# The projections of a two-layer mixer and expert block: three float32r products a step, or one float32 product

## The chip, the cores and the metric

The kernel runs on one core of a Trainium2 chip. The metric is the device time of one execution in microseconds (us), the median of several runs. The engines are named as the profile names them: PE (TensorE, the matrix products, with its weight loads as PEld), DVE (VectorE), ACT (ScalarE), POOL (GpSimd) and SP (SyncE, which here only issues DMA loads).

## The reference, cut to what matters

The input is 256 tokens of 1024 channels in float32. Two layers follow one another, and each has two halves:

```python
h = modulate(rms_norm(x, g_mix[l]), sh1, sc1)
x = x + g1 * token_mixers(h, pos, w_in[l], ..., w_o[l])
h = modulate(rms_norm(x, g_ffn[l]), sh2, sc2)
x = x + g2 * grouped_moe(h, w_router, b_router, w_gate[l], w_up[l], w_down[l])

def token_mixers(h, pos, w_in, w_dw, b_dw, ln_g, ln_b, w_o):
    proj = h @ w_in                                   # 256 x 1024 by 1024 x 2340
    cu, cg, dq, dk, dv, iq, ik, iw, mq, mk, mv = jnp.split(proj, offs, axis=-1)
    y_conv = conformer_conv(cu, cg, w_dw, b_dw, ln_g, ln_b)   # 31 taps, 256 channels
    ...                                               # rope on dq, dk, iq, ik, mq, mk
    y_dsa = dsa_attention(dq, dk, dv, iq, ik, iw)     # 6 heads; each query keeps its top 64 keys
    y_moba = moba_attention(mq, mk, mv)               # 6 heads; one block here, so causal
    return jnp.concatenate([y_conv, y_dsa, y_moba], axis=-1) @ w_o    # 1024 x 1024
```

The vectors `sh1`, `sc1`, `g1` and their like come from a product of `silu(c)` with `w_ada`. `grouped_moe` runs 16 experts with gate, up and down matrices; a router gives each token two of them. The two products of `token_mixers`, with `w_in` and with `w_o`, are what the change touches.

## The kernel before

Time goes through these stages: the product with `w_ada`, the mixers of layer 0 (about 35 to 169 us in the profile), the experts of layer 0, the mixers of layer 1 (about 324 to 459 us), the experts of layer 1, and the last norm.

**Weights.** All of them (181 MB, float32) pass through one ring of 14 slots of SBUF. The list `loads` fixes their order. `pump()` lets SP issue the next load (L77) as long as a slot is free, and `done(key)` gives a slot back once all that read it have read it, and pumps again. A mixer stage takes from the ring two slots of `ix`, eight slots of 256 columns of `w_in` (`cu`, `cg`, `d0`, `d1`, `q0`, `q1`, `m0`, `m1`) and four slots of `w_o`; an expert pair takes four slots of gate and up and two of `w_down`. The loads of the experts come right behind those of the mixers.

**Split products.** The mixers' products are in the type float32r. An operand is split in a high part, its cast to float32r, and a low part, what the cast leaves of it, and three products stand for one: high by high, high by low, low by high. For weights `split()` does it: ACT casts a piece of the ring slot to `WH` (L404), POOL subtracts that from the slot and leaves `WL` (L405). Each has four buffers.

```python
S.copy(WH, w)
G.tensor_tensor(WL, w, WH.bitcast(F32), OP.subtract)
```

The activations are split where they are made: `hH` on ACT (L416), `hL` on DVE (L417). The mixers' results go the same way into `yH` and `yL`, in `Pair.value` (L567, L568) and behind the convolution (L729, L730).

**Products of the mixers.** `proj` makes tokens by columns, `proj_T` (for `cu` and `cg`) columns by tokens. Each goes over eight rows of 128 (`k`) and two blocks of the result, which are 16 steps of three products each (L442 to L444, L459 to L461). A product has 256 columns, in `ix` 292. `out_part(k)` adds the part of `w_o` that belongs to row block `k` of the result `y` to eight accumulators: eight steps of three products (L664 to L666), and eight parts in a layer, so 64 steps.

**Attention.** Results of a projection are copied from PSUM by ACT, turned by the rope on DVE (`rope_in_place`, L474 to L477, two blocks of tokens with four operations each), transposed on PE (`transposes`, L483) and copied into the buffer `QK` by DVE (L484). A `Pair` is two heads: `score` (the products in `score_mm`, L493 and L495, and the softmax, whose row minima are DVE's at L533, exponentials ACT's at L536, reciprocal DVE's at L539, scaling DVE's at L543), `flip` (transposes of the probabilities on PE, L551) and `value`. For the dsa heads `select_keys` first finds the top 64 scores of each query in eight rounds on DVE. `score_mm` has the index products as well.

**Convolution.** Its 31 taps are DVE operations over 256 columns, for two blocks of channels (the first tap of a block at L692, the others at L694, together 56 in a layer). The last six taps of the second block are POOL's: one product (L681), then five sums (L685) of terms that ACT makes (L684); they are called `rest` and are added at L700. A mean over channels (L706, L718) is a float32 product on PE.

**What sets the order.** In `mixers` the order on PE is that of the code, by hand: `ix`, `cu`, transposes of the index heads, `cg`, the index scores, then `d0`, `d1`, `q0`, first flip, `q1`, second flip, `early.take` (products with `w_ada` for a later stage), third flip, `dsa[0].score`, `m0`, and so on, at the end the parts of the output projection with flips and scores of the moba heads between them. The order on DVE, ACT and POOL is set by a scheduler when the program is built, by its own costs; the taps have no place of their own and fill in where it thinks that DVE has nothing else. In the expert stage the orders of PE and of DVE are both by hand.

Of the kernel before, what the change touches and what calls it, by code (L numbers as in the profile page):

```python
# [52 lines left out]
def block_kernel(ctx: ExitStack, tc: tile.TileContext, x, c, w_ada, b_ada, g_mix, w_in, w_dw, b_dw, ln_conv_g,  # L53
# [346 lines left out]

    def split(wk, w, shape):
        WH = wk.tile(shape, F32R, name="WH", tag="WH", bufs=4)
        WL = wk.tile(shape, F32R, name="WL", tag="WL", bufs=4)
        S.copy(WH, w)  # L404
        G.tensor_tensor(WL, w, WH.bitcast(F32), OP.subtract)  # L405
        return WH, WL

    def mixers(big, wk, l, norm, early):
        a1, sh1 = mod["sc1", l], mod["sh1", l]
        rs = norm.rs  # L410
        hH = big.tile([P, KT, SEQ], F32R, name="hH", tag="H")
        hL = big.tile([P, KT, SEQ], F32R, name="hL", tag="L")
        for k in range(KT):
            t = wk.tile([P, SEQ], F32, name="ht", tag="ht")
            V.scalar_tensor_tensor(out=t, in0=xT[:, k, :], scalar=a1[:, k:k + 1], in1=rs, op0=OP.mult, op1=OP.mult)
            S.activation(hH[:, k, :], t, AF.Identity, bias=sh1[:, k:k + 1])  # L416
            V.scalar_tensor_tensor(out=hL[:, k, :], in0=t, scalar=sh1[:, k:k + 1], in1=hH[:, k, :].bitcast(F32),  # L417
                                   op0=OP.add, op1=OP.subtract)
        QK = big.tile([P, 10, SEQ], F32, name="QK")
# [7 lines left out]
        def proj(name, w=256):  # L427
            if w <= 256:
                pp = bank([P, NT, w])
                pts = [pp[:, t, :] for t in range(NT)]  # L430
            else:
                pts = [bank([P, w]) for _ in range(NT)]
                pp = pts
            for kh in range(4):
                WH, WL = split(wk, w_rows(name, 2 * kh), [P, 2, w])
                for kk in range(2):
                    k = 2 * kh + kk
                    for t in range(NT):
                        tt = slice(t * P, (t + 1) * P)
                        first = k == 0 and (w > 256 or t == 0)  # L440
                        last = k == KT - 1 and (w > 256 or t == NT - 1)
                        T.matmul(pts[t], hH[:, k, tt], WH[:, kk, :], start=first, stop=False)  # L442
                        T.matmul(pts[t], hH[:, k, tt], WL[:, kk, :], start=False, stop=False)  # L443
                        T.matmul(pts[t], hL[:, k, tt], WH[:, kk, :], start=False, stop=last)  # L444
                if name == "ix" and kh % 2 == 1:
                    done(("win", l, "ix", kh // 2))
            if name != "ix":
                done(("win", l, name))
            return pp

        def proj_T(name):
            pp = bank([P, 2, SEQ])
            for kh in range(4):
                WH, WL = split(wk, w_rows(name, 2 * kh), [P, 2, 256])
                for kk in range(2):
                    k = 2 * kh + kk
                    for cc in range(2):
                        cs = slice(cc * P, (cc + 1) * P)
                        T.matmul(pp[:, cc, :], WH[:, kk, cs], hH[:, k, :], start=(k == 0 and cc == 0), stop=False)  # L459
                        T.matmul(pp[:, cc, :], WH[:, kk, cs], hL[:, k, :], start=False, stop=False)  # L460
                        T.matmul(pp[:, cc, :], WL[:, kk, cs], hH[:, k, :], start=False, stop=(k == KT - 1 and cc == 1))  # L461
            done(("win", l, name))
# [55 lines left out]
        class Pair:  # L518
# [40 lines left out]
            def value(self):  # L559
# [4 lines left out]
                for i, v in enumerate((va, vb)):  # L564
                    T.matmul(po[64 * i:64 * i + 64, P:2 * P], v[1], self.pts[i][:, 2 * P:3 * P], start=False,
                             stop=True)
                S.copy(yH[:, dst, :], po)  # L567
                V.tensor_tensor(yL[:, dst, :], po, yH[:, dst, :].bitcast(F32), OP.subtract)  # L568

# [66 lines left out]
        pp = proj("m1")  # L636
        yH = big.tile([P, KT, SEQ], F32R, name="yH", tag="H")
        yL = big.tile([P, KT, SEQ], F32R, name="yL", tag="L")
        S.copy(VV[:, :, HD:HD + 256], pp)
# [17 lines left out]
        def out_part(k):  # L657
            ki = nk[0]
            for n in range(KT):
                if n % 4 == 0:  # L660
                    WH, WL = split(wk, wt["wo", l, k // 2][:, k % 2, n * P:(n + 4) * P], [P, 512])
                ns = slice((n % 4) * P, (n % 4 + 1) * P)
                po = pos[n // 2][:, n % 2, :]
                T.matmul(po, WH[:, ns], yH[:, k, :], start=(ki == 0 and n % 2 == 0), stop=False)  # L664
                T.matmul(po, WH[:, ns], yL[:, k, :], start=False, stop=False)  # L665
                T.matmul(po, WL[:, ns], yH[:, k, :], start=False, stop=(ki == KT - 1 and n % 2 == 1))  # L666
            nk[0] += 1
# [55 lines left out]
        for cc in range(2):  # L723
# [4 lines left out]
        V.scalar_tensor_tensor(out=yc, in0=th, scalar=1.0, in1=yc, op0=OP.add, op1=OP.mult)  # L728
        S.activation(yH[:, 0:2, :], yc, AF.Copy, scale=0.5)  # L729
        V.scalar_tensor_tensor(out=yL[:, 0:2, :], in0=yc, scalar=0.5, in1=yH[:, 0:2, :].bitcast(F32), op0=OP.mult,  # L730
                               op1=OP.subtract)
        out_part(4)
# [603 lines left out]
```

## Time and profile before

| | us |
|---|---|
| three runs | 607.84, 608.03, 612.25 |
| their median | 608.03 |
| the profiled execution | 609.77 |
| its span (first to last instruction) | 608.1 |
| mean granted clock of PE in it | 0.946 |
| PE busy | 535.8 |
| DVE busy | 348.2 |
| ACT busy | 215.8 |
| POOL busy | 181.1 |

The profiled execution is 1.7 us longer than its span, and 0.3% longer than the median of the runs. The costliest line on POOL is L405, the subtraction, with 138.0 us in 104 operations; on ACT it is L404, the cast, with 62.5 us. The products of L442 to L444 and L664 to L666 are float32r; those of `score_mm`, the transposes and the means are float32. A group of equal instructions that follow one another is drawn together in a timeline row, with its count (x12), and the time from the start of the first to the end of the last. A float32 product is recorded as two matmuls, so two products stand there as x4. The granted clock is a share of the full one, 2.4 GHz; the lower level is 1.2 GHz, so 0.5.

### The profile page before, as it was taken

To read this page: it belongs to the slowest core of one execution; us is meant where nothing else is said; L and a number is where in the kernel's file an instruction comes from. 1 tells how busy PE (TensorE), PEld (TensorE's weight loads), DVE (VectorE), ACT (ScalarE), POOL (GpSimd) and SP (SyncE) were. 2 spreads that over 40 slices of the span, in tenths; PEclk is the share of its full clock that TensorE was granted. 3 is DMA by queue.
4 is the path that set the end of the run, shared out by engine and by line. 5 is a ranking of instruction groups with operands and counts; after the bars stand their busy time and mean duration, and the time that the engine had idled before them with its cause. 6 is when DMAs were issued, how large, how long until landed. Compare 5 with 4: busy or idle time off the path is not lost. (4 is left out here: it accounts for less than half of the span.)

```text
span 608.1 us, 11533 instructions
## 1 busy us (share of the span) xinstructions
PE 535.8 (88%) x4297; PEld 341.3 (56%) x4297; DVE 348.2 (57%) x912; ACT 215.8 (35%) x472; POOL 181.1 (30%) x155
## 2 busy tenths in 40 slices
PE   2788979599979999999968997697998899999993
PEld 0268975468945355555436797383895444444431
DVE  1275899987575332333237689999756733333323
ACT  0353713366661212111146372244676121111114
POOL 1056738333630000000005775533362011111110
PEclk9788979699998999999978997898999899999998
DMA  8999988948289999999999998745637699999952
GB/s 319 380 304 386 393 321 314 376 137 265 87 254 365 365 359 359 357 358 362 391 362 370 386 386 325 274 141 152 213 120 215 219 349 354 363 357 356 360 202 73
DMA packets 126027, 182.85 MB, mean 301 GB/s; under 512 B 7920, under 2 KB 94216, under 8 KB 125960
## 3 DMA queue, kind: packets, MB, share of 16 engines
q1 hardware_dynamic: 125344, 180.80, 86.2%
q10 hardware_dynamic: 616, 1.19, 0.5%
q8 instruction: 38, 0.62, 0.4%
q14 instruction: 29, 0.24, 0.1%
HBM read 180.92 MB, written 1.05 MB: 299 GB/s over the span
## 5 line engine op out<-in xcount | busy, mean ns | idle before, releaser
L405 POOL TENSOR_TENSOR WL<-w,WH 128x512 fp32r<-128x512 f32 (+1 forms) x104 | 138.0, 1355 | 141.7 <-ACT WH L404 123.7
L979 PE MATMUL bank<-w,XT 128*32 128x512 f32 (+1 forms) x1024 | 112.9, 592 | 0.0
L404 ACT CAST WH<-w 128x512 fp32r<-128x512 f32 (+1 forms) x104 | 62.5, 624 | 43.5 <-PE bank L460 19.1
L979 PEld LDWEIGHTS bank<-w,XT 128*32 128x32 f32 x1024 | 33.5, 110 | 75.1 <-issue 68.4
L444 PE MATMUL bank<-WH,hL 128*128 128x256 f32 (+1 forms) x224 | 68.7, 307 | 3.0 <-DVE hL L417 2.8
L442 PE MATMUL bank<-WH,hH 128*128 128x256 f32 (+1 forms) x224 | 69.1, 308 | 1.0 <-ACT hH L416 0.9
L443 PE MATMUL bank<-WL,hH 128*128 128x256 f32 (+1 forms) x224 | 68.0, 303 | 1.2 <-POOL WL L405 1.2
L694 DVE SCALAR_TENSOR_TENSOR cvy<-cva,hw,cvy 128x256 f32<-128x256 f32 x108 | 59.3, 594 | 0.5
L1017 PE MATMUL bank<-w,eaT 128*32 128x512 f32 (+1 forms) x512 | 58.2, 595 | 0.4
L967 DVE SCALAR_TENSOR_TENSOR eac<-eth,bank 128x256 f32<-128x256 f32 x16 | 6.7, 422 | 83.4 <-ACT eth L966 83.4
L275 PE MATMUL bank<-w,cB 128*32 128x512 f32 x384 | 51.3, 652 | 3.1 <-DMA w<-in_w_ada 1.2
L444 PEld LDWEIGHTS bank<-WH,hL 128*128 128x128 f32 x224 | 46.6, 208 | 4.9 <-DVE hL L417 4.9
L442 PEld LDWEIGHTS bank<-WH,hH 128*128 128x128 f32 x224 | 47.2, 211 | 3.7 <-ACT hH L416 2.0
L443 PEld LDWEIGHTS bank<-WL,hH 128*128 128x128 f32 x224 | 46.9, 209 | 1.4 <-POOL WL L405 1.4
L1005 POOL TENSOR_TENSOR Yl<-yf,Yh 128x512 fp32r<-128x512 f32 x14 | 18.0, 1287 | 95.0 <-ACT Yh L1004 95.0
L966 ACT ACTIVATE eth<-bank 128x256 f32<-128x256 f32 x16 | 6.1, 384 | 96.2 <-PE bank L979 96.2
L1184 POOL MEMSET rc<- 128x4 f32 x2 | 0.2, 102 | 131.3 <-ACT warm L259 131.3
L664 PE MATMUL bank<-yH,WH 128*128 128x256 f32 x128 | 37.0, 289 | 0.0
L665 PE MATMUL bank<-yL,WH 128*128 128x256 f32 x128 | 35.8, 280 | 0.0
L666 PE MATMUL bank<-yH,WL 128*128 128x256 f32 x128 | 35.8, 280 | 0.0
L957 PE MATMUL bank<-D,gH 128*128 128x256 f32 x128 | 33.5, 299 | 2.4 <-DVE eac L967 2.4
L536 ACT ACTIVATE pr<-pr,nm 128x128 f32<-128x128 f32 (+1 forms) x48 | 21.3, 445 | 39.4 <-DVE nm L533 39.4
(287 smaller groups left out, 1026.4 us busy)
## 6 DMA issues: line engine op xcount, KB each, us to landing
w<-in_w_ada SPq DMA_DIRECT2D x48, 1024.0 KB, 12.0
w<-in_w_gate SPq DMA_DIRECT2D x128, 256.0 KB, 6.2
w<-in_w_up SPq DMA_DIRECT2D x128, 256.0 KB, 6.0
w<-in_w_down SPq DMA_DIRECT2D x64, 512.0 KB, 7.8
w<-in_w_in SPq DMA_DIRECT2D x16, 1024.0 KB, 13.1
w<-in_w_o SPq DMA_DIRECT2D x8, 1024.0 KB, 8.8
w<-in_w_in SPq DMA_DIRECT2D x4, 328.0 KB, 15.0
xin<-in_x ACTq DMA_DIRECT2D x1, 1024.0 KB, 9.8
```

Source lines behind the costliest of these rows:

```text
L275: T.matmul(self.pa[j:j + 32, :], cB[:, 2 * kq + kk, o:o + 32], W[:, kk, h * 512:(h + 1) * 512], start=(u == 0 and kq == 0), stop=(u + 1 == ...
L404: S.copy(WH, w)
L405: G.tensor_tensor(WL, w, WH.bitcast(F32), OP.subtract)
L442: T.matmul(pts[t], hH[:, k, tt], WH[:, kk, :], start=first, stop=False)
L443: T.matmul(pts[t], hH[:, k, tt], WL[:, kk, :], start=False, stop=False)
L444: T.matmul(pts[t], hL[:, k, tt], WH[:, kk, :], start=False, stop=last)
L664: T.matmul(po, WH[:, ns], yH[:, k, :], start=(ki == 0 and n % 2 == 0), stop=False)
L665: T.matmul(po, WH[:, ns], yL[:, k, :], start=False, stop=False)
L666: T.matmul(po, WL[:, ns], yH[:, k, :], start=False, stop=(ki == KT - 1 and n % 2 == 1))
L694: tap = V.scalar_tensor_tensor(out=cy[:, cc, :], in0=src, scalar=w, in1=cy[:, cc, :], op0=OP.mult, op1=OP.add)
L979: T.matmul(pf[b0:b0 + BLK, :], XT[:, k, o + b0:o + b0 + BLK], W[:, e, k % 2, :], start=(k == 0), stop=(k == KT - 1))
L1017: T.matmul(pd[b0:b0 + BLK, :], aT[:, f, b0:b0 + BLK], W[:, e, f, :], start=(f == 0), stop=(f == 1))
```

## The change

`split()` goes, with its casts on ACT and its subtractions on POOL. `hH` and `hL` become one float32 tensor `hT`, `yH` and `yL` one float32 tensor `yT`, and DVE's operations that made `hL` and `yL` go as well. Each step of `proj`, `proj_T` and `out_part` is one float32 product, and its weight operand is the ring slot itself.

```diff
--- before.py
+++ after.py
@@ -398,24 +398,14 @@
         norm.add(k)
 
 
-    def split(wk, w, shape):
-        WH = wk.tile(shape, F32R, name="WH", tag="WH", bufs=4)
-        WL = wk.tile(shape, F32R, name="WL", tag="WL", bufs=4)
-        S.copy(WH, w)
-        G.tensor_tensor(WL, w, WH.bitcast(F32), OP.subtract)
-        return WH, WL
-
     def mixers(big, wk, l, norm, early):
         a1, sh1 = mod["sc1", l], mod["sh1", l]
         rs = norm.rs
-        hH = big.tile([P, KT, SEQ], F32R, name="hH", tag="H")
-        hL = big.tile([P, KT, SEQ], F32R, name="hL", tag="L")
+        hT = big.tile([P, KT, SEQ], F32, name="hT", tag="H")
         for k in range(KT):
             t = wk.tile([P, SEQ], F32, name="ht", tag="ht")
             V.scalar_tensor_tensor(out=t, in0=xT[:, k, :], scalar=a1[:, k:k + 1], in1=rs, op0=OP.mult, op1=OP.mult)
-            S.activation(hH[:, k, :], t, AF.Identity, bias=sh1[:, k:k + 1])
-            V.scalar_tensor_tensor(out=hL[:, k, :], in0=t, scalar=sh1[:, k:k + 1], in1=hH[:, k, :].bitcast(F32),
-                                   op0=OP.add, op1=OP.subtract)
+            S.activation(hT[:, k, :], t, AF.Identity, bias=sh1[:, k:k + 1])
         QK = big.tile([P, 10, SEQ], F32, name="QK")
         VV = big.tile([P, NT, 7 * HD], F32, name="VV")
 
@@ -432,16 +422,14 @@
                 pts = [bank([P, w]) for _ in range(NT)]
                 pp = pts
             for kh in range(4):
-                WH, WL = split(wk, w_rows(name, 2 * kh), [P, 2, w])
+                W = w_rows(name, 2 * kh)
                 for kk in range(2):
                     k = 2 * kh + kk
                     for t in range(NT):
                         tt = slice(t * P, (t + 1) * P)
                         first = k == 0 and (w > 256 or t == 0)
                         last = k == KT - 1 and (w > 256 or t == NT - 1)
-                        T.matmul(pts[t], hH[:, k, tt], WH[:, kk, :], start=first, stop=False)
-                        T.matmul(pts[t], hH[:, k, tt], WL[:, kk, :], start=False, stop=False)
-                        T.matmul(pts[t], hL[:, k, tt], WH[:, kk, :], start=False, stop=last)
+                        T.matmul(pts[t], hT[:, k, tt], W[:, kk, :], start=first, stop=last)
                 if name == "ix" and kh % 2 == 1:
                     done(("win", l, "ix", kh // 2))
             if name != "ix":
@@ -451,14 +439,13 @@
         def proj_T(name):
             pp = bank([P, 2, SEQ])
             for kh in range(4):
-                WH, WL = split(wk, w_rows(name, 2 * kh), [P, 2, 256])
+                W = w_rows(name, 2 * kh)
                 for kk in range(2):
                     k = 2 * kh + kk
                     for cc in range(2):
                         cs = slice(cc * P, (cc + 1) * P)
-                        T.matmul(pp[:, cc, :], WH[:, kk, cs], hH[:, k, :], start=(k == 0 and cc == 0), stop=False)
-                        T.matmul(pp[:, cc, :], WH[:, kk, cs], hL[:, k, :], start=False, stop=False)
-                        T.matmul(pp[:, cc, :], WL[:, kk, cs], hH[:, k, :], start=False, stop=(k == KT - 1 and cc == 1))
+                        T.matmul(pp[:, cc, :], W[:, kk, cs], hT[:, k, :], start=(k == 0 and cc == 0),
+                                 stop=(k == KT - 1 and cc == 1))
             done(("win", l, name))
             return pp
 
@@ -564,8 +551,7 @@
                 for i, v in enumerate((va, vb)):
                     T.matmul(po[64 * i:64 * i + 64, P:2 * P], v[1], self.pts[i][:, 2 * P:3 * P], start=False,
                              stop=True)
-                S.copy(yH[:, dst, :], po)
-                V.tensor_tensor(yL[:, dst, :], po, yH[:, dst, :].bitcast(F32), OP.subtract)
+                S.copy(yT[:, dst, :], po)
 
         def heads(name, nrope, tail=None):
             pp = proj(name)
@@ -634,8 +620,7 @@
         dsa[1].score()
         dsa[0].flip()
         pp = proj("m1")
-        yH = big.tile([P, KT, SEQ], F32R, name="yH", tag="H")
-        yL = big.tile([P, KT, SEQ], F32R, name="yL", tag="L")
+        yT = big.tile([P, KT, SEQ], F32, name="yT", tag="H")
         S.copy(VV[:, :, HD:HD + 256], pp)
         dsa[0].value()
         flip2(QK[:, 4:6, :], p4)
@@ -656,14 +641,10 @@
 
         def out_part(k):
             ki = nk[0]
+            W = wt["wo", l, k // 2][:, k % 2, :]
             for n in range(KT):
-                if n % 4 == 0:
-                    WH, WL = split(wk, wt["wo", l, k // 2][:, k % 2, n * P:(n + 4) * P], [P, 512])
-                ns = slice((n % 4) * P, (n % 4 + 1) * P)
-                po = pos[n // 2][:, n % 2, :]
-                T.matmul(po, WH[:, ns], yH[:, k, :], start=(ki == 0 and n % 2 == 0), stop=False)
-                T.matmul(po, WH[:, ns], yL[:, k, :], start=False, stop=False)
-                T.matmul(po, WL[:, ns], yH[:, k, :], start=False, stop=(ki == KT - 1 and n % 2 == 1))
+                T.matmul(pos[n // 2][:, n % 2, :], W[:, n * P:(n + 1) * P], yT[:, k, :],
+                         start=(ki == 0 and n % 2 == 0), stop=(ki == KT - 1 and n % 2 == 1))
             nk[0] += 1
             if k % 2 == 1:
                 done(("wo", l, k // 2))
@@ -726,9 +707,7 @@
         th = t2k([P, 2, SEQ], "th")
         S.activation(th, yc, AF.Tanh, scale=0.5)
         V.scalar_tensor_tensor(out=yc, in0=th, scalar=1.0, in1=yc, op0=OP.add, op1=OP.mult)
-        S.activation(yH[:, 0:2, :], yc, AF.Copy, scale=0.5)
-        V.scalar_tensor_tensor(out=yL[:, 0:2, :], in0=yc, scalar=0.5, in1=yH[:, 0:2, :].bitcast(F32), op0=OP.mult,
-                               op1=OP.subtract)
+        S.activation(yT[:, 0:2, :], yc, AF.Copy, scale=0.5)
         out_part(4)
         blk[1].value()
         blk[2].flip()
```

PE's order by hand stays, step by step. The scheduler's order on DVE is another one. Two places of it are shown, both in the mixers of layer 0; in a row `x12` is twelve equal instructions in a row.

The first is DVE between the first two flips of the dsa heads: `ropa`, `ropb` and `pb` belong to the rope of `q0` and `q1`, `cvy` rows are taps of the convolution, and the `QK` row is the copy of the second flip, on which `dsa[0].score` waits. Before:

```order
L477 TENSOR_TENSOR pb<-ropa,ropb 128x4x16
L694 SCALAR_TENSOR_TENSOR cvy<-cva,hw,cvy 128x256 x12
L474 TENSOR_TENSOR ropa<-pb,ropet 128x64
L475 TENSOR_TENSOR ropb<-pb,ropet 128x4x8
L476 TENSOR_TENSOR ropb<-pb,ropet 128x4x8
L474 TENSOR_TENSOR ropa<-pb,ropet 128x64
L477 TENSOR_TENSOR pb<-ropa,ropb 128x4x16
L475 TENSOR_TENSOR ropb<-pb,ropet 128x4x8
L476 TENSOR_TENSOR ropb<-pb,ropet 128x4x8
L484 COPY QK<-bank_986 128x512
L477 TENSOR_TENSOR pb<-ropa,ropb 128x4x16
L694 SCALAR_TENSOR_TENSOR cvy<-cva,hw,cvy 128x256 x16
```

And with the change:

```order
L464 TENSOR_TENSOR pb<-ropa,ropb 128x4x16
L675 SCALAR_TENSOR_TENSOR cvy<-cva,hw,cvy 128x256 x15
L461 TENSOR_TENSOR ropa<-pb,ropet 128x64
L462 TENSOR_TENSOR ropb<-pb,ropet 128x4x8
L463 TENSOR_TENSOR ropb<-pb,ropet 128x4x8
L461 TENSOR_TENSOR ropa<-pb,ropet 128x64
L464 TENSOR_TENSOR pb<-ropa,ropb 128x4x16
L462 TENSOR_TENSOR ropb<-pb,ropet 128x4x8
L463 TENSOR_TENSOR ropb<-pb,ropet 128x4x8
L471 COPY QK<-bank_641 128x512
L464 TENSOR_TENSOR pb<-ropa,ropb 128x4x16
L675 SCALAR_TENSOR_TENSOR cvy<-cva,hw,cvy 128x256 x12
```

Taps moved forward: here 15 stand where 12 stood, and with those further up 37 of them stand ahead of the `QK` copy instead of 23.

The second place is DVE from the end of the softmax of `dsa[0]` to the next copy of a flip. Before:

```order
L533 ISA nm 128x1
L694 SCALAR_TENSOR_TENSOR cvy<-cva,hw,cvy 128x256 x3
L539 RECIPROCAL sums<-sums 128x4
L694 SCALAR_TENSOR_TENSOR cvy<-cva,hw,cvy 128x256
L543 TENSOR_SCALAR pr<-pr,sums 128x128
L543 TENSOR_SCALAR pr<-pr,sums 128x256
L543 TENSOR_SCALAR pr<-pr,sums 128x128
L543 TENSOR_SCALAR pr<-pr,sums 128x256
L694 SCALAR_TENSOR_TENSOR cvy<-cva,hw,cvy 128x256 x6
L484 COPY QK<-bank_1149 128x512
```

And with the change:

```order
L520 ISA nm 128x1
L526 RECIPROCAL sums<-sums 128x4
L530 TENSOR_SCALAR pr<-pr,sums 128x128
L530 TENSOR_SCALAR pr<-pr,sums 128x256
L530 TENSOR_SCALAR pr<-pr,sums 128x128
L530 TENSOR_SCALAR pr<-pr,sums 128x256
L471 COPY QK<-bank_756 128x512
```

The ten taps between the minima and the copy have gone from here; they stand ahead of the softmax now.

## Rows read from the trace of the kernel before

**Rows 1.** The page: busy us of each engine, share of the span, instructions.

```profile
PE 535.8 (88%) x4297; PEld 341.3 (56%) x4297; DVE 348.2 (57%) x912; ACT 215.8 (35%) x472; POOL 181.1 (30%) x155
```

**Rows 2.** Stretches: us; busy PE, PEld, DVE, ACT, POOL; granted clock, DMA share, GB/s.

```profile
186.00:302.00 116.00, 114.54 (x1013) 56.32 (x1013) 39.75 (x89) 22.07 (x41) 0.00 (x0) 0.99 1.08 364
```

**Rows 3.** Timeline of PE, output projection: start us, length us; first and last product.

```profile
157.42 0.38 PE L664 MATMUL bank<-yH,WH 128*128 128x256 f32 x1
...
168.65 0.28 PE L666 MATMUL bank<-yH,WL 128*128 128x256 f32 x1
```

**Rows 4.** Timeline of PE and its loads, float32 products: [idle before, releaser] at the end.

```profile
148.32 1.13 PE L718 MATMUL bank<-cs,mean_c 128*128 128x256 f32 x4
...
431.29 0.70 PE L706 MATMUL bank<-cvy,mean_c 128*128 128x256 f32 x2
...
598.28 0.19 PEld L1038 LDWEIGHTS bank<-Yf,DT 128*128 128x128 f32 x1 [0.24 <-issue]
```

**Rows 5.** Waits of PE, 34 to 460 us: us in total, times, longest.

```profile
PE bank L551 <- DVE pr L543: 10.4, 9, 4.2
PE bank L483 <- DVE pb L477: 7.3, 4, 3.3
PE bank L493 <- DVE QK L484: 5.2, 1, 5.2
...
PE bank L444 <- DVE hL L417: 2.8, 4, 1.3
PE bank L483 <- DVE pi L477: 1.9, 2, 1.1
...
PE bank L443 <- POOL WL L405: 1.2, 1, 1.2
```

**Rows 6.** Stretches of the mixer stages, columns as in rows 2.

```profile
36.00:45.40 9.40, 8.42 (x47) 7.57 (x48) 7.92 (x15) 4.91 (x12) 6.12 (x5) 0.82 1.10 348
53.60:61.00 7.40, 7.40 (x54) 7.27 (x52) 0.69 (x1) 1.91 (x4) 3.34 (x3) 0.77 1.02 408
83.60:91.50 7.90, 7.90 (x51) 7.90 (x50) 7.90 (x32) 0.00 (x0) 0.00 (x0) 0.70 0.60 239
117.40:125.50 8.10, 8.10 (x50) 8.00 (x48) 7.36 (x28) 3.52 (x11) 1.25 (x1) 0.69 0.46 155
324.00:334.00 10.00, 8.50 (x48) 7.67 (x49) 8.26 (x14) 6.08 (x13) 5.34 (x5) 0.83 1.08 363
373.20:381.30 8.10, 8.10 (x51) 8.10 (x49) 8.10 (x25) 1.86 (x3) 4.19 (x3) 0.67 0.48 188
416.00:420.00 4.00, 4.00 (x22) 1.71 (x26) 3.79 (x14) 1.00 (x5) 0.00 (x0) 0.57 0.69 208
```

**Rows 7.** Timeline of DVE: start us, length us of the group.

```profile
89.42 4.84 DVE L694 SCALAR_TENSOR_TENSOR cvy<-cva,hw,cvy 128x256 f32<-128x256 f32 x12
94.18 0.22 DVE L474 TENSOR_TENSOR ropa<-pb,ropet 128x64 f32<-128x64 f32 x1
...
365.07 4.49 DVE L474 TENSOR_TENSOR ropa<-pb,ropet 128x64 f32<-128x64 f32 x1
...
378.01 1.33 DVE L475 TENSOR_TENSOR ropb<-pb,ropet 128x32 f32<-128x32 f32 x1
...
382.18 8.70 DVE L694 SCALAR_TENSOR_TENSOR cvy<-cva,hw,cvy 128x256 f32<-128x256 f32 x12
...
410.82 5.11 DVE L543 TENSOR_SCALAR pr<-pr,sums 128x128 f32<-128x128 f32 x4
...
434.91 1.01 DVE L543 TENSOR_SCALAR pr<-pr,sums 128x128 f32<-128x128 f32 x4
```

**Rows 8.** The last w_down of layer 0: its issue, its landing (page), its first use.

```profile
288.30 2.53 SPq L77 DMA_DIRECT2D w<-in_w_down  x4
...
w<-in_w_down SPq DMA_DIRECT2D x64, 512.0 KB, 7.8
...
302.61 0.64 PE L1017 MATMUL bank<-w,eaT 128*32 x4
```

## Prediction

> **What bounds the kernel now.** I read the totals by engine first [rows 1]: PE, the matmul engine, is busy for 535.8 of 608.1 us, DVE for 348.2, POOL for 181.1. A total cannot say where PE is the limit, so next comes the view by stretches. In the expert stage of layer 0 [rows 2] PE is busy for 114.54 of 116 us and POOL for nothing: PE sets its length, and nothing in it changes; layer 1's looks the same. Before each expert stage lies a mixer stage, about 35 to 169 us and 324 to 459 us, and all edits are there. PE leads there too: it runs its products back to back and then stands still for some microseconds. The view of waits [rows 5] names whom it stands for, nearly always DVE. And during or after most of these pauses the view by stretches shows a mean granted clock of 0.57 to 0.83 [rows 6], so part of the products then run at 1.2 instead of 2.4 GHz. A mixer stage lasts as long as PE's products, PE's waits, and what the low clock adds. The change makes the first longer and can take from the other two; the forecast is the balance.
>
> **Part 1: the products get dearer.** Today one k step is three float32r products. From the first to the last of 96 such products in the output projection 11.23 us pass [rows 3], so 0.118 us each and 0.354 us for three. A float32 product is recorded as two matmuls, each with its own weight load. The row of one such product with 256 columns (line 706) lasts 0.70 us, that of two in a row (line 718) 1.13 us [rows 4]: the second costs 0.43 us, which with four passes over 256 columns at 2.4 GHz is 0.427 us. So a step grows by 0.427 - 0.354 = 0.073 us. A layer has 128 steps in eight projections of 256 columns and 64 in the output projection: 192 x 0.073 = 14.0 us. The projection "ix" has 16 steps of 292 columns; scaled by 292/256 a step goes from 0.404 to 0.487 us, together 1.3 us. That is 15.3 us a layer, **30.6 us in all**, all on PE, which is the path. The two rows are rounded to 0.01 us, so the step may cost 0.42 to 0.45 us: 3 us less or 9 us more.
>
> Here a rule stands against the row. The float32 load in [rows 4] lasts 0.19 us and is followed by 0.24 us in which the load path idles, while the products run on; loads are hidden. The Trainium skill, TensorE: Matmul & The Clock Gate, section "The mechanism" of Part 3, says that a weight load overlaps a running matmul only when it goes to another row group, which these full-height products never do. By that rule every load would lie open; the sum goes by the row, and the rule is behind the last rival.
>
> **Part 2: casts and subtractions go.** ACT loses 104 casts, POOL 104 subtractions, DVE the hL and yL operations. Off PE's path they are worth nothing by themselves, and PE waits for them little: 1.2 us for WL and 2.8 us for hL in both layers [rows 5]. ACT's casts I cost at nothing: ACT delays PE nowhere by more than a microsecond.
>
> What POOL's silence is worth is DVE's speed. Four scalings (line 543) take 1.01 us at 434.91, where POOL is idle, and 5.11 us at 410.82, beside four subtractions. Twelve conv taps take 4.84 us at 89.42 and 8.70 us at 382.18. A rope operation takes 0.22 us at 94.18, 1.33 us at 378.01 (one of four such rows around it) and 4.49 us at 365.07 [rows 7]. In all the long rows POOL works, in the short ones not. POOL keeps the six "rest" operations of lines 681 and 685 in each layer.
>
> **Part 3: the waits.** For DVE: 10.4 + 7.3 + 5.2 + 2.8 + 1.9 us, for POOL 1.2 us: 28.8 us in 21 waits [rows 5]. Behind each the pipeline fills again: a product takes 0.28 us to its end where in a row one comes every 0.118 [rows 3], so 21 x 0.16 = 3.4 us. Low clock: a stretch of s us with mean granted clock c loses about s x (1 - c). Layer 0: 9.4 x 0.18 + 7.4 x 0.23 + 7.9 x 0.30 + 8.1 x 0.31 = 8.3 us; layer 1: 10 x 0.17 + 8.1 x 0.33 + 4 x 0.43 = 6.1 us [rows 6]. So 28.8 + 3.4 + 14.4 = **46.6 us** can go at most.
>
> Does it go? The point that decides is the first dsa score, which needs DVE's copy of the second flip into QK; in layer 1 PE waits 5.2 us for it today. In DVE's new order 37 conv taps stand ahead of that copy, 23 before: 14 x 0.403 = 5.6 us later. Against that DVE gains ahead of it 8.70 - 4.84 = 3.9 us on the taps, 4.3 us on the rope at 365.07 and some 4 us on the four ropes [rows 7]: 12.2, net 6.6 us earlier. PE gets there later by four projections of 16 x 0.073 = 1.17 us, 4.7 us, and earlier by half of the 7.3 us of line 477 and by the 2.7 us of low clock: 1.7 us earlier. So the wait there goes from 5.2 to 5.2 - 6.6 + 1.7 = 0.3 us, plus what POOL's rest adds, which run just then, cost DVE: between nothing and 4 us. I take 2 us for each layer, 4 us in all. The next waits, for line 543, should be gone: the conv taps between reciprocal and scalings were moved ahead, and four scalings cost 1.01 us. The output projection has no wait today and gets none: its operand yT is ready one DVE operation earlier.
>
> **Part 4: the ring.** A w_in or w_o slot was free when POOL had subtracted, now when PE has multiplied. POOL was ahead by at most four WL buffers, two parts of the output projection, some 6 us. In the expert stage the slots are taken faster than filled, so such a lag would last until its end: the last w_down of layer 0 is issued from 288.30 to 290.8, lands 7.8 us later and is used at 302.61 [rows 8], a slack of 4 us. The most that the lag can cost is 2 us a layer; I take nothing, since the transfers stand still for part of the mixer stage anyway.
>
> **Sum.** 30.6 - 46.6 + 4 = -12.0 us. The profiled execution took 609.8 us, 608.1 in the span and 1.7 around it, 0.3% over the median of the runs, 608.0. So 597.8 by it and 596.0 by the median: I say **596 us**; 591 to 601 for this case alone.
>
> **The rivals.** *All waits go*: 30.6 - 46.6 = -16, 592 us, and some less where shorter slow stretches vanish too, 590. For it: the 0.3 us worked out above. Chance 0.17.
>
> *The clock does not hold.* Low clock came after waits of under 2 us too (the stretch from 53.6). If my 2 us waits bring it again, two stretches in each layer lose 2 us: 596 + 8 = 604. Chance 0.10.
>
> *The weights come late* by the 2 us of part 4 in each layer: 600. For it: the thin slack. Against: it is positive. Chance 0.10.
>
> *The waits stay and it gets slower.* If DVE's long rows are not POOL's doing, the waits for lines 543, 477 and 484 (22.9 us) and the low clock behind them (9.3 us) stay, and the 14 taps at 0.725 us (8.70/12) put the QK copy up to 10.2 us later in each layer. Of the 46.6 us 14.4 go; the waits swallow 11.7 us of the 30.6 (ten projections). That is +4.5, and up to 20.4 more: about +15, 623 us. It decides from a mean tap of some 0.55 us on. Against it: long and short rows part cleanly by POOL. Chance 0.07.
>
> *The float32 loads are not hidden*: 832 loads x 0.19 us = 158 us on top, some 754 us. [rows 4] speaks against it. The Trainium skill's page of part 1 is what stands for it. Chance 0.01.
>
> The forecast has 0.53; the last 0.02 are anything near today's time. Some 1% (6 us) is what a measurement of this kernel can tell from no change, its three runs lying between 607.8 and 612.3 us. Faster by over 1% (below 602): the forecast, the first rival, most of the late weights and some of the clock case, 0.82. Within 1%: 0.11. Slower: 0.07. The range 587 to 606 leaves out the slow cases and the ends of a product's price.
>
> **What would show it.** A float32 step of 0.427 us, so 3.42 us for the eight of an output part; conv taps near 0.40 us except beside the rest adds; four scalings in about 1 us; PE's waits for lines 477 and 543 gone and 0 to 4 us left for the QK copy; granted clock near 1.0 from the index scores to the end of the stage; both mixer stages about 6 us shorter, the expert stages as long as today. I am wrong if taps stay near 0.6 us, if a step costs more than 0.45 us, or if PE waits for transfers in the expert stages.

## The result

The changed kernel takes 593.22 us (median of four runs, 592.91 to 593.65), the kernel before 609.49 (four runs, one more than in the table above, 607.84 to 612.25). The ratio is 0.973, 95% interval 0.969 to 0.977: faster, by 16 us. The profiled execution took 593.65 us, its span 591.9.

### The profile after

The page's first part answers to [rows 1]: PE is busy for 14 us more in a span that is 16 us shorter, and POOL for 135 us less.

```profile
PE 549.9 (93%) x3881; PEld 334.9 (57%) x3881; DVE 278.5 (47%) x882; ACT 158.6 (27%) x368; POOL 46.0 (8%) x51
```

Next the two mixer stages as stretches, from the first product of `ix` to the end of the last of the output projection, columns as in [rows 2]. Of the kernel before:

```profile
34.90:168.90 134.00, 119.50 (x914) 101.43 (x917) 109.52 (x298) 65.56 (x153) 74.37 (x58) 0.91 0.80 290
323.80:459.20 135.40, 119.46 (x914) 99.70 (x914) 112.93 (x297) 66.71 (x154) 72.40 (x57) 0.94 0.73 256
```

And of the changed one:

```profile
36.00:160.00 124.00, 123.99 (x702) 96.90 (x702) 76.75 (x283) 38.46 (x104) 7.32 (x6) 1.00 0.84 305
315.60:440.40 124.80, 124.73 (x702) 97.22 (x702) 76.28 (x282) 39.16 (x106) 7.54 (x6) 1.00 0.77 273
```

PE stood still for 14.5 + 15.9 = 30.4 us of the two stages and now for 0.1; its granted clock was 0.91 and 0.94 and is 1.00. Its waits from 30 to 450 us answer to [rows 5]:

```profile
PE bank L804 <- DVE slb L788: 4.0, 1, 4.0
PE bank L1023 <- PEq L1170: 3.7, 1, 3.7
PE bank L936 <- DVE eac L946: 1.3, 1, 1.3
PE bank L432 <- ACT hT L408: 1.1, 2, 0.9
```

Every wait for ropes, QK copies and scalings is gone; the first three lines are outside the mixers and were there before, the fourth stands ahead of the first products of `ix`. PE's timeline of the output projection answers to [rows 3] and gives the price of a float32 step: the last four parts have 32 steps, and 160.06 - 146.05 = 14.01 us pass, 0.438 us each.

```profile
146.05 14.08 PE L646 MATMUL bank<-yT,w 128*128 128x256 f32 x64
160.06 1.06 PE L275 MATMUL bank<-w,cB 128*32 128x512 f32 x8
```

And DVE's timeline answers to [rows 7]: taps at 0.40 us each (5.63/14), except twelve at 0.62 that ran beside POOL's rest, a rope operation at 0.22, four scalings at 1.01.

```profile
77.61 5.63 DVE L675 SCALAR_TENSOR_TENSOR cvy<-cva,hw,cvy 128x256 f32<-128x256 f32 x14
83.15 0.22 DVE L461 TENSOR_TENSOR ropa<-pb,ropet 128x64 f32<-128x64 f32 x1
92.53 7.43 DVE L675 SCALAR_TENSOR_TENSOR cvy<-cva,hw,cvy 128x256 f32<-128x256 f32 x12
102.91 1.01 DVE L530 TENSOR_SCALAR pr<-pr,sums 128x128 f32<-128x128 f32 x4
```

Where the time went, stage by stage, in us of the profiled executions (borders are the starts of the first `ix` product and of the last output product; the last column is all that follows):

| kernel | start | mixers 0 | experts 0 | mixers 1 | experts 1, end | span |
|---|---|---|---|---|---|---|
| before | 34.9 | 133.7 | 155.2 | 135.1 | 149.1 | 608.1 |
| changed | 36.0 | 123.7 | 155.9 | 124.4 | 151.8 | 591.9 |
| subtractions and casts back | 35.0 | 151.5 | 154.9 | 153.9 | 151.0 | 646.3 |
| subtractions back | 38.1 | 146.7 | 157.8 | 131.3 | 152.0 | 625.8 |
| before, zeros for WL | 35.4 | 112.9 | 158.2 | 113.6 | 149.0 | 569.1 |
| output split, POOL subtracts | 36.4 | 122.5 | 156.7 | 124.4 | 150.4 | 590.4 |
| output split, DVE subtracts | 34.8 | 119.5 | 156.3 | 120.3 | 150.2 | 581.1 |

The mixers gave 10.0 + 10.7 us; 1.1, 0.7 and 2.7 us were lost again outside them.

### The profile page after: what moved, and what is told of

Read it like the earlier page. It is cut to its first block, busy times and chain, and to the rows that moved or that the text cites. A ratio compares the mean times of both kernels' runs of the same rounds, so it can differ in the third digit from the quotient of the medians.

```text
span 591.9 us, 10356 instructions
## 1 busy us (share of the span) xinstructions
PE 549.9 (93%) x3881; PEld 334.9 (57%) x3881; DVE 278.5 (47%) x882; ACT 158.6 (27%) x368; POOL 46.0 (8%) x51
## 5 line engine op out<-in xcount | busy, mean ns | idle before, releaser
L958 PE MATMUL bank<-w,XT 128*32 128x512 f32 (+1 forms) x1024 | 112.9, 592 | 0.0
L432 PE MATMUL bank<-w,hT 128*128 128x256 f32 (+1 forms) x448 | 100.9, 385 | 1.1 <-ACT hT L408 1.1
L432 PEld LDWEIGHTS bank<-w,hT 128*128 128x128 f32 x448 | 84.3, 190 | 16.3 <-ACT hT L408 2.1
L646 PE MATMUL bank<-yT,w 128*128 128x256 f32 x256 | 57.5, 381 | 0.0
L646 PEld LDWEIGHTS bank<-yT,w 128*128 128x128 f32 x256 | 48.0, 190 | 6.9 <-issue 0.7
L996 PEld LDWEIGHTS bank<-w,eaT 128*32 128x32 f32 x512 | 15.2, 109 | 32.0 <-issue 28.9
L936 PE MATMUL bank<-D,gL 128*128 128x256 f32 x128 | 31.6, 285 | 0.0
L940 ACT ACTIVATE XT<-bank,sh,sc 128x256 f32<-128x256 f32 x36 | 18.2, 561 | 44.6 <-PE bank L936 44.6
L936 PEld LDWEIGHTS bank<-D,gH 128*128 128x128 f32 x128 | 25.0, 195 | 7.0 <-issue 5.0
L447 PE MATMUL bank<-hT,w 128*128 128x256 f32 x128 | 28.3, 379 | 0.0
L447 PEld LDWEIGHTS bank<-hT,w 128*128 128x128 f32 x128 | 24.2, 190 | 3.3
L936 PEld LDWEIGHTS bank<-D,gL 128*128 128x128 f32 x128 | 25.0, 195 | 0.0
```

Of the source, the lines that this page charges most:

```text
L432: T.matmul(pts[t], hT[:, k, tt], W[:, kk, :], start=first, stop=last)
L447: T.matmul(pp[:, cc, :], W[:, kk, cs], hT[:, k, :], start=(k == 0 and cc == 0), stop=(k == KT - 1 and cc == 1))
L646: T.matmul(pos[n // 2][:, n % 2, :], W[:, n * P:(n + 1) * P], yT[:, k, :], start=(ki == 0 and n % 2 == 0), stop=(ki == KT - 1 and n % 2 == 1))
L936: T.matmul(pg[:, i, :], z[:, t, ks], D[:, t, :], start=(si == 0), stop=(si == 3))
L940: S.activation(XT[:, k, :], pg[:, i, :], AF.Identity, bias=sh2[:, k:k + 1], scale=a2[:, k:k + 1])
L958: T.matmul(pf[b0:b0 + BLK, :], XT[:, k, o + b0:o + b0 + BLK], W[:, e, k % 2, :], start=(k == 0), stop=(k == KT - 1))
```

## The experiments

The theory: POOL's subtractions slow DVE, PE's waits were that slowness, and the change pays some 30 us on PE to be rid of them. Two rivals: the waits went because DVE's order is new and it has fewer operations; or because PE comes later now. The first runs cross products and POOL's work while DVE's order stays the same but for a few taps.

**Subtractions and casts back, unread.**

```diff
                 W = w_rows(name, 2 * kh)
+                split(wk, W, [P, 2, w])       # in proj, proj_T and out_part; nobody reads it
```

> The changed kernel with the 104 casts on ACT and the 104 subtractions on POOL put back as idle work: their results are read by nobody, the products stay float32 and read the ring slot. DVE's order stays that of the changed kernel but for a few taps. Theory (POOL's subtractions slow DVE, and PE's waits for DVE were that): conv taps beside POOL go from 0.40 to 0.6 us or more, four scalings from 1 to some 5 us, PE's waits for DVE's ropes, QK copies and scalings come back with stretches of low clock behind them; 600 to 615 us. Rival 1 (DVE's new order or its fewer operations took the waits away): 593 us within 3. Rival 2 (PE comes later because its products got dearer, so DVE's delay stays hidden): DVE's rows get longer but PE waits under 3 us in all, 593 to 597 us.

Measured: 647.85 us (647.49 to 649.94), ratio 1.063 (1.057 to 1.068). The direction is the theory's, the size is not. DVE's timeline has the same fourteen taps as above, at 1.04 us instead of 0.40:

```profile
87.75 14.54 DVE L686 SCALAR_TENSOR_TENSOR cvy<-cva,hw,cvy 128x256 f32<-128x256 f32 x14
```

The waits of PE and of ACT (us in total, times, longest) tell why it is worse than before: a part is ACT, which stands before its casts until POOL gives back a buffer (27.5 us; in the kernel before 2.3), with the transposed probabilities that PE waits for queued behind it.

```profile
PE bank L489 <- DVE QK L480: 16.8, 2, 9.8
PE bank L559 <- ACT pT L550: 9.7, 3, 5.1
```

```profile
ACT WH L404 <- POOL WL L405: 27.5, 44, 0.8
```

**Casts alone, subtractions alone.** The same edit with only `S.copy(WH, w)`, or with only `G.tensor_tensor(WL, w, w, OP.subtract)`, in `split`.

> The changed kernel with the 104 casts on ACT put back alone, read by nobody; no subtraction. Theory (the casts cost PE nothing): 593 us within 3, DVE's rows as in the changed kernel. Rival (the casts stand ahead of ACT's copies and exponentials and were part of what PE waited for): 598 us or more, with waits of PE or DVE on ACT.

> The changed kernel with the 104 subtractions on POOL put back alone (slot minus slot, read by nobody), no casts on ACT. With both back the time was 647.9 us, with the casts alone 592.9. Theory (POOL's work slows DVE by itself): groups of taps beside POOL last twice as long or more, PE waits for DVE come back; 605 to 640 us. Rival (what cost so much was ACT standing still for POOL's buffers ahead of its copies, not DVE being slowed): 593 to 598 us, taps near 0.40 us.

Measured: casts alone 592.87 us (588.90 to 594.82), no change; subtractions alone 627.56 (626.59 to 634.52), ratio 1.032 (1.026 to 1.038). So POOL's work costs 34 us without ACT, and with ACT's casts ahead of it 20 more. This is not the price of the subtractions where the kernel before had them: they wait for hardly more than the loads here, they are shorter (1.08 us in the mean, 1.36 before), and they run at other times. In layer 0 the sixteen for `w_o` run in a row beside the taps and ropes that stand ahead of the second flip's copy, and PE waits for that copy:

```profile
103.49 17.27 POOL L403 TENSOR_TENSOR WL<-w 128x512 fp32r<-128x512 f32 x16 [0.61 <-DMA w<-in_w_o]
```

```profile
PE bank L486 <- DVE QK L477: 12.1, 1, 12.1
```

In layer 1 fourteen of the sixteen start at 409.95, behind the copy (401.06). PE stood still for 16.7 us in the first stage and 3.1 in the second, and low clock took some 6 and 3 us: the 23 and 7 us by which the two stages are longer. DVE by line, 34 to 480 us (busy us, mean ns of one, idle before). Before:

```profile
L694 DVE SCALAR_TENSOR_TENSOR cvy<-cva,hw,cvy 128x256 f32<-128x256 f32 x108 | 59.3, 594 | 0.5
L543 DVE TENSOR_SCALAR pr<-pr,sums 128x128 f32<-128x128 f32 (+1 forms) x48 | 25.5, 594 | 0.2
L511 DVE MAX8 m<-isc 128x8 f32<-128x128 f32 (+1 forms) x32 | 9.8, 349 | 0.0
L484 DVE COPY QK<-bank 128x512 f32<-128x512 f32 x12 | 8.2, 682 | 1.1 <-PE bank L483 1.1
```

The changed kernel:

```profile
L675 DVE SCALAR_TENSOR_TENSOR cvy<-cva,hw,cvy 128x256 f32<-128x256 f32 x108 | 49.8, 511 | 0.6
L530 DVE TENSOR_SCALAR pr<-pr,sums 128x128 f32<-128x128 f32 (+1 forms) x48 | 12.1, 315 | 0.3
L498 DVE MAX8 m<-isc 128x8 f32<-128x128 f32 (+1 forms) x32 | 9.7, 344 | 0.0
L471 DVE COPY QK<-bank 128x512 f32<-128x512 f32 x12 | 8.2, 687 | 23.7 <-PE bank L470 23.6
```

With the subtractions alone put back:

```profile
L683 DVE SCALAR_TENSOR_TENSOR cvy<-cva,hw,cvy 128x256 f32<-128x256 f32 x108 | 58.5, 591 | 0.6
L536 DVE TENSOR_SCALAR pr<-pr,sums 128x128 f32<-128x128 f32 (+1 forms) x48 | 15.2, 382 | 0.3
L504 DVE MAX8 m<-isc 128x8 f32<-128x128 f32 (+1 forms) x32 | 9.8, 348 | 0.0
L477 DVE COPY QK<-bank 128x512 f32<-128x512 f32 x12 | 8.2, 685 | 9.0 <-PE bank L476 9.0
```

Taps and scalings follow POOL; MAX8 and the copies out of PSUM don't, in any of the three. Laid over POOL's operations, the trace of the kernel before has 15 of the 48 scalings beside POOL, at 1.21 us in the mean, and 31 away from it, at 0.31; all its 32 MAX8 ran beside POOL, at 0.35 us, and none of the changed kernel's did, at 0.34. It is no general slowness of DVE. The Trainium skill, SBUF — State Buffer, section "SBUF: two separate sides", has a pair of ports that DVE and GpSimd hold in turn for a whole instruction, which a DVE operation needs if it has two SBUF inputs or runs in a two-port mode. The trace agrees in kind. The rope operation of 1.33 us [rows 7] starts at 378.01 inside one subtraction and ends at 379.34, 0.04 us behind it; the next slow one runs from 379.51 to 380.82 and ends 0.08 us behind the next subtraction:

```profile
376.88 2.42 POOL L405 TENSOR_TENSOR WL<-w,WH 128x512 fp32r<-128x512 f32 x1 [5.92 <-ACT WH L404]
379.43 1.31 POOL L405 TENSOR_TENSOR WL<-w,WH 128x512 fp32r<-128x512 f32 x1
```

POOL seems to wait for DVE too: the first of these two began beside two taps and took 2.42 us, and the first operation of `rest` took 0.93 us at 382.15 in the kernel before and 3.48 and 3.77 us in the changed one. No run took that apart.

**The kernel before, without subtractions.** The second product multiplies zeros, so the low part of the weights is left out.

```diff
-        G.tensor_tensor(WL, w, WH.bitcast(F32), OP.subtract)
+        WL = zero if len(shape) == 2 else zero.rearrange("p (k n) -> p k n", k=2)
```

> The kernel before, three float32r products a step, DVE's order as before but for some taps, without the subtractions: the second product multiplies a tensor of zeros, so the low part of the weights is left out. Theory (POOL's silence alone takes the waits away): PE's waits for lines 477, 484 and 543 of before fall from 22.9 us to under 8 us, and the products stay at some 0.36 us a step: 562 to 575 us. Rival (the waits went because dearer products make PE later): the waits stay above 15 us, 590 to 605 us.

Measured: 571.29 us (570.00 to 571.84), ratio 0.936 (0.932 to 0.940). With DVE's old order and PE early, the waits of the mixers are 4.9 us, where [rows 5] has 22.9:

```profile
PE bank L554 <- DVE pr L546: 2.6, 1, 2.6
PE bank L496 <- DVE QK L487: 2.3, 1, 2.3
```

Both rivals fall: POOL's silence alone takes the waits away. (An earlier form, expected at 565 to 577 us, put `WH` in for `WL`. That nearly doubles the products, the experts' overflow branch ran, and its 797 us say nothing on the question.)

**Where the cheap products can stay.** The output projection as before, in the changed kernel; then with `V` for `G` in `split`, so that DVE subtracts.

```diff
+        G.tensor_tensor(WL, w, WH.bitcast(F32), OP.subtract)   # first run; second run: V.tensor_tensor
-                T.matmul(pos[n // 2][:, n % 2, :], W[:, n * P:(n + 1) * P], yT[:, k, :], ...)
+                T.matmul(po, WH[:, ns], yH[:, k, :], ...)      # and yL by WH, yH by WL
```

> The changed kernel with the output projection alone as before: 16 casts and 16 subtractions a layer, yH and yL, three float32r products a step. Theory: 64 steps a layer go from 0.438 back to 0.354 us, 5.4 us a layer; before had nearly no wait there, so about 583 us, 581 to 587. Rival (the subtractions slow the softmax and the end of the convolution on DVE, or WL comes late): waits of PE for DVE or POOL in the output projection eat it, 589 to 595 us.

> The changed kernel with the whole output projection as three float32r products, as in the run with its subtractions on POOL (588.3 us), but with the 16 subtractions a layer on DVE and nothing new on POOL. Theory (what that run lost against the 5.4 us a layer of its cheaper products was DVE slowed by POOL): taps and scalings keep the lengths of the changed kernel, PE waits for DVE under 1 us in all, 582 to 586 us. Rival (16 subtractions of some 0.7 us and the yL operations in DVE's own order delay the softmax and the end of the convolution as much): 587 to 592 us, with waits of PE for DVE in the output projection.

Measured: with POOL 588.29 us (585.34 to 592.11), a little over its range; with DVE 583.20 (582.41 to 585.37), ratio to before 0.957 (0.954 to 0.959). The intervals of the ratios, 0.957 to 0.968 and 0.954 to 0.959, still touch; in the traces the mixers are 7.1 us shorter with DVE (table), though DVE has more to do. Of these, 1.7 us are `ix` of layer 0, which ran partly at the low clock in the trace with POOL (9.82 us instead of 8.13); it did so in the traces of both pads below too, so that is not POOL's doing. PE stood still for 2.7 us in the two stages with POOL, nearly all of it for scalings. With DVE the subtraction takes 0.69 us, and PE waits in neither mixer stage:

```profile
34.80:154.50 119.70, 119.66 (x766) 96.52 (x766) 88.68 (x305) 46.47 (x119) 7.65 (x6) 1.00 0.90 326
310.70:431.00 120.30, 120.30 (x766) 96.79 (x766) 87.75 (x304) 46.95 (x120) 7.54 (x6) 1.00 0.81 288
```

Two variants of that. Only the last four parts split:

> The changed kernel with the last four parts of the output projection (rows 6, 7, 0, 1) as three float32r products, their casts on ACT and their subtractions on DVE, which has little to do there; nothing new on POOL. Theory: 32 steps a layer go from 0.438 to some 0.36 us, 2.5 us a layer, no new wait: 588 us, 587 to 590. Rival (the subtractions stand in DVE's order ahead of the end of the convolution, and PE waits for that or for WL): 592 to 596 us.

Measured: 589.27 us (587.42 to 591.88), as expected. And `cu` and `cg` split too:

> The run with the whole output projection split and subtracted on DVE (583.2 us), and the same for the projections cu and cg as well: eight casts more of the activations on ACT and eight hL on DVE, eight casts and eight subtractions of weights a layer, three buffers of WH and two of WL. Theory (three products are cheaper wherever DVE has time to subtract): 32 steps a layer go from 0.438 to some 0.36 us, 2.5 us a layer, DVE stands nearly idle in that stretch: 577 to 580 us. Rival (the subtractions stand ahead of the ropes of the index heads on DVE, or the casts of the activations make PE wait at the start of ix, and low clock follows; or two buffers of WL are too few in the output projection): 582 to 588 us.

Measured: 582.00 us (579.34 to 584.96), ratio 0.954 (0.951 to 0.958): a miss, in the rival's range, and it cannot be told from 583.2. `cu` and `cg` got cheaper (6.1 and 6.0 us instead of 7.1), but the output projection waited twice for `WL` (2.1 us) with two buffers, and `ix` of layer 0 ran partly at the low clock, as in other traces without this edit.

**The end of the kernel.** Behind the last expert stands a branch, and from the last expert product to the end 12.6 us passed before and 15.2 after. PE and ACT there, of the kernel before (the last column is the idle time ahead, and its releaser):

```profile
597.85 1.88 PE L1038 MATMUL bank<-Yf,DT 128*128 128x512 f32 x4
```

```profile
597.82 1.28 ACT L259 ACT_TABLE_LOAD   x1 [2.49 <-ACTq L1191]
```

After:

```profile
579.24 0.39 PE L1017 MATMUL bank<-Yl,DT 128*128 128x512 f32 x1
581.50 3.44 PE L1017 MATMUL bank<-Yf,DT 128*128 128x512 f32 x4 [1.87 <-issue]
```

```profile
580.27 1.28 ACT L259 ACT_TABLE_LOAD   x1 [3.72 <-ACTq L1170]
```

PE pauses for 1.87 us in the middle of its last products, waiting for nothing that the profile shows, and the rest runs at half speed (granted clock 0.52 from 581.5 to 585 us); ACT starts 1.2 us later than before.

```diff
+        pad = bank([P, P])
+        for _ in range(6):
+            T.transpose(pad, ident, ident)    # second run: and 40 x S.copy(padt, eps_t) on ACT
```

> The changed kernel with six more transposes of a constant on PE, 24 or so instructions, placed in an early stretch in which PE waits for a load anyway; everything behind them stands that much further on in PE's program. After the last expert PE's trace shows a pause of 1.87 us with nothing to wait for, some ten instructions behind a branch, and products at the low clock behind it. Theory (that pause is PE's program being fetched, and where it falls depends on where the branch's target stands): the pause goes or moves, the end of the kernel is 2 to 3.5 us shorter, 590 to 591.5 us. Rival (the pause belongs to the work, not to the place in the program): 593 us within 0.7, pause as long as before.

> The changed kernel with six transposes more on PE and 40 copies of one column more on ACT, all early, where both engines wait for loads. The end of the kernel, from the last expert product on, took 15.2 us in the changed kernel, 14.5 with the six transposes alone; there ACT came 3.6 to 3.7 us after that product in the three runs with 368 instructions counted on ACT, and 2.3 to 2.6 us after it where ACT had 384 or more. Theory (where ACT's program stands behind the last branch sets that too): ACT comes after some 2.5 us, the end takes 12.5 to 13.2 us, the kernel 590 to 591.5 us. Rival (ACT's lateness has another cause): 3.6 us and 14.5 us stay.

Measured: 591.96 us (588.80 to 593.56) and 590.21 (588.47 to 591.46). Six products and six loads more on PE, and the pause is gone; but ACT was as late as in the changed kernel, so the end took 14.5 us, 0.7 less where 2 to 3.5 was expected. With the copies ACT came earlier, and it took 13.4.

```profile
579.64 0.40 PE L1020 MATMUL bank<-Yl,DT 128*128 128x512 f32 x1
579.88 1.88 PE L1020 MATMUL bank<-Yf,DT 128*128 128x512 f32 x4
```

```profile
578.95 1.28 ACT L265 ACT_TABLE_LOAD   x1 [2.80 <-PE bank L1023]
```

So the pause goes with where the code stands, as far as one trace of each kernel can tell: the four traces with 3881 products counted on PE all have it (0.74 to 1.87 us, not always at the same product), the two with 3887 don't. The gain in the medians is 1 and 3 us. The first is less than such a kernel differs from run to run. For the second, all five runs lie under the four of the changed kernel, but the intervals of the ratios to before, 0.964 to 0.969 and 0.969 to 0.977, touch.

## Why the prediction held, and where its terms were off

The forecast was 596 us with 591 to 601 for its own case; 593.2 lies in it. The mechanism was the one named, and three terms were off: the products cost 3 us more than in the sum, waits and clock gave 12 us more, and the sum had nothing for the 4.5 us lost outside the mixers. That these partly cancel is luck.

- **The products.** 0.427 us a step was too low: 0.438 measured (14.01/32). Against (168.86 - 157.42)/32 = 0.358 before, a step grows by 0.080, not 0.073: about 34 us with `ix`, not 30.6. The loads are hidden, as [rows 4] had it: PE comes through a step, which has two loads of 0.19 us, in 0.438 us. The sentence of the Trainium skill on row groups (TensorE: Matmul & The Clock Gate, "The mechanism" of Part 3) does not hold for these products; the same section also lets a load into the background weight buffer go ahead of running products, and that fits.
- **The waits and the clock.** 46.6 us were to go and 4 to stay. What went is 20.7 us of the stages and the 34 us that the products took: some 54. Idle time is 30.4 us of it, where I counted 28.8. Low clock is about 18 (busy time times what the clock lacked, over stretches of 1 us), where the picked stretches gave 14.4; the rest, some 6 us, was not taken apart (the sum had 3.4 for refilling the pipeline). Nothing stayed.
- **The step that failed** is the 2 us a layer for the QK copy. It was worked out from layer 1 and charged to both layers; but in layer 0 PE asked 3.7 us after the copy ended already before, and [rows 5] counts one such wait. In layer 1 PE's request came 3.2 us earlier in the stage (the sum had 1.7) and the copy's end 9.7 us earlier (the sum had 6.6). So in layer 0 the copy now ends at 92.4 us and PE asks for it at 95.5, with all 37 taps ahead of it; in layer 1 the times are 374.5 and 375.8, with 39 (25 before; the 37 and 23 are layer 0's). POOL's `rest`, for which the 2 us stood, put no add ahead of the copy: the adds start at 91.79 and 374.73, and the taps ahead took 0.40 us each. The rows are below. The rival "all waits go" (592 us) was nearer the truth than the forecast.
- **A row misread.** The twelve taps of 8.70 us at 382.18 [rows 7] ran beside six operations of `rest` and one subtraction. The change keeps `rest`, so this row could not show what POOL's silence is worth; the taps got their 0.40 us because in layer 1 the adds of `rest` moved behind them. Nor is POOL idle in all the short rows: the rope operation at 94.18 lies inside the first operation of `rest` (92.19, 3.06 us). The rows of the scalings, beside subtractions alone, carried the argument.
- **What the sum had not** is the start and the end: +1.1 us in the first loads, which differ from run to run (34.7 to 38.1 us in these kernels), and +2.6 at the end. Without them the time would have been under 590, outside the 591 to 601.

The QK copy and the request of the kernel before in layer 0, and in layer 1 the first operation of `rest` and the request (its wait at the end):

```profile
95.23 0.68 DVE L484 COPY QK<-bank 128x512 f32<-128x512 f32 x1
99.60 0.49 PE L493 MATMUL bank<-QK 64*128 64x128 f32 x4
382.15 0.93 POOL L681 TENSOR_SCALAR rest<-cva,hw 128x256 f32<-128x256 f32 x1
392.35 0.80 PE L493 MATMUL bank<-QK 64*128 64x128 f32 x4 [5.17 <-DVE QK L484]
```

And of the changed kernel, layers 0 and 1, with the first add of `rest` in layer 1:

```profile
91.70 0.68 DVE L471 COPY QK<-bank 128x512 f32<-128x512 f32 x1
95.49 0.49 PE L480 MATMUL bank<-QK 64*128 64x128 f32 x4
373.76 0.69 DVE L471 COPY QK<-bank 128x512 f32<-128x512 f32 x1
374.73 0.78 POOL L666 TENSOR_TENSOR rest<-rest,term 128x256 f32<-128x256 f32 x1
375.83 0.49 PE L480 MATMUL bank<-QK 64*128 64x128 f32 x4
```

The other rivals: the clock held, at 1.00. No wait for a transfer appeared in the expert stages, so weights did not come late. That DVE's long rows were not POOL's doing is refuted by the runs with subtractions put back. The casts were worth nothing, as said: 592.87 us with all of them. What would show it was shown: taps at 0.40 us but beside the rest, four scalings at 1.01, waits gone, clock 1.00; only "both stages about 6 us shorter" was too little, 10.0 and 10.7.

What stays open: why the end after both pads still takes 0.8 us more than before, why `ix` of layer 0 ran partly at the low clock in some traces, and what the kernel before would take with all its subtractions on DVE, which was not run.

## What to carry to other kernels

An engine with a third of the busy time can set the length of a stage by slowing its neighbour: compare the same operation's rows beside it and away from it, before looking at orders and waits. A dearer product on the engine that sets the time paid off here, since it bought the others' silence; but in the output projection, where DVE has room, it was not needed. There cheap products with the subtraction on DVE are better still: 583 us, and 582, which cannot be told from it, with `cu` and `cg` as well. That the other projections need the dearer product, because DVE has no room beside them, is argued and not shown.

## What the runs showed of the hardware

A DVE operation with two inputs in SBUF, or a scaling by a column, can last as long as the POOL subtraction beside it: four scalings take 1.01 us away from POOL and 5.11 us beside four subtractions [rows 7], while MAX8 keeps its 0.35 us.

A branch can cost more or less with the number of instructions ahead of it, as far as one trace of each kernel shows. ACT came 3.6 to 3.7 us after the last expert product in the three kernels with 368 instructions counted on it, and 2.3 to 2.6 in those with 384 or more; PE's pause of 1.87 us went with six products and their loads. The Trainium skill, Runtime: NRT & Kernel Launch, section "Instruction fetch mechanics", says that a program is fetched in blocks and that a taken branch has to wait when its target is not in the blocks at hand. That fits; no run here shows a block, or that the time is spent on fetching.
